# Where the queries of a dilated attention kernel are put into block order, and how early

## The chip, the cores and the metric

The kernel runs on one core of one Trainium2 chip. The metric is the device time of one execution in microseconds. Names of the engines: PE is TensorE (matmuls; PEld its weight loads), DVE is VectorE, ACT is ScalarE, POOL is GpSimd, SP is SyncE, which here issues the DMAs. All data is float32. A measurement of this kernel can tell a difference of about 0.3% from no change.

## What is computed

One layer of a decoder with two attention mixers side by side, for a prompt of 2048 tokens and 8 single sample tokens. What matters here is mixer A on the prompt: each of 8 heads is evaluated in three strided patterns, and the three partial outputs are merged by their softmax denominators. Mixer B is an ordinary window of 128 (dilation 1) with a learned sink per head.

```python
DILATED_CONFIGS = ((128, 1), (512, 4), (2048, 16))

def _band_partial(q, k, v):
    # q, k, v cut into blocks of 128; each block of queries sees its own and the previous block of keys
    sc = jnp.einsum('nbqhgd,nbkhd->nbhgqk', qb, kk) * (HEAD_DIM ** -0.5)
    sc = jnp.where(valid[None, :, None, None], sc, -jnp.inf)
    m = sc.max(-1)
    p = jnp.exp(sc - m[..., None])
    den = p.sum(-1)
    o = jnp.einsum('nbhgqk,nbkhd->nbqhgd', p, vv).reshape(n, L, hk, g, dh)
    ...
    return m, den, o

def _prompt_layer(x, w_in, sinks, w_o, ln_g, ln_b):
    ...
    qa, ka, va, ga, qb, kb, vb, gb = _project(x, pos, w_in)
    parts = []
    for _, d in DILATED_CONFIGS:
        m, den, o = _band_partial(_dilate(qa[:, :, :, None], d), _dilate(ka, d), _dilate(va, d))
        parts.append((_undilate(m, b, s, d), _undilate(den, b, s, d), _undilate(o, b, s, d)))
    oa = _merge(parts)
    ...
    y = _output(x, oa, ob, ga, gb, w_o, ln_g, ln_b)
```

## The kernel before

The kernel runs in three stages. Up to about 400 us it projects keys, part of the queries and the values. Then comes the attention stage, which the change touches, up to about 1000 us. At the end stands the output projection with its normalization.

**Batches.** The attention stage works on pairs of heads: four pairs of mixer A, then four of mixer B. A pair of A has three jobs, with dilation 16, 4 and 1; a pair of B has one, with dilation 1. A job has 16 blocks of 128 queries, worked on in four batches of four blocks. That makes 16 jobs and 64 batches, numbered 0 to 63 here: 0 to 3 are dilation 16 of the first pair, 4 to 7 its dilation 4, 8 to 11 its dilation 1, 12 to 15 dilation 16 of the second pair, and so on; 48 to 63 are mixer B.

**Queries in block order.** A pair's queries lie in SBUF as a tile `q` of 128 x 2048, loaded by four DMAs (L906), in an order of tokens that suits dilation 16. For that dilation the scores read `q` directly. For dilations 4 and 1 the queries of a batch are first copied into a tile `qo` of 128 x 512, in the order of the blocks; this is `fetch_q` (L789 to L801), with the copy itself in L800. There are two buffers of `qo`. So 48 of the 64 batches need such a copy.

**A pipeline of batches, in an order written out by hand.** In step i of the loop at L1121 come the scores of batch i on PE (L823), the products with the values of batch i-2 (L874), the masked minimum (L831, DVE) and the exponential (L834, ACT) of batch i, and, in four slots, the transposes of batch i-1 (L853, PE) with their evictions `pT` (L859 on DVE, each fourth on ACT). Into the slots PE's remaining work is strewn by `advance`: projections of the gates and of mixer B's queries (L629), later the first part of the output projection. In slot 1 of step i stands `fetch_q` for batch i+1 (L1143). Each engine gets its instructions in the order in which this code issues them (`manual_schedule`), SP with its DMAs too.

**POOL in this stage.** When the third job of a pair of A is done, `merge_a` (L1001) joins the three partial outputs in eight chunks of 256 tokens. Each chunk needs a tile `F` of three weights, spread over 64 partitions each, which two DMAs fetch from DRAM (L1038); `F` has two buffers. A chunk is five instructions on POOL (one L1050, two each of L1052 and L1053), and between chunks lie two slots, in which the fetch for the chunk after next is issued. The merge of a pair falls into the steps of the next pair's dilation 4 and 1. POOL also splits weights into a high and a low part (L137, L138: `gw`, `gw2h`, `gw3h`, `wl`, `wo`), for which it waits for their loads and for the last matmul that read the buffer, and it copies the sample tokens' gates (L174, `sgS`).

**SP in this stage** issues in order: `F`, the projection's inputs `gx` (L581), keys, queries and values of the next job (L898, L906, L772 to L782), weights (L142), and the stores of gates (L175), queries (L200) and merged outputs (L1058).

Of the kernel before, what the change touches and what calls it, by code (L numbers as in the profile page):

```python
# [51 lines left out]
def hymba_step(ctx, tc, xt, xs, xr, wq, wv, wo, tab, msk, ident, diag, sinks, lng, lnb,  # L52
               kca, vca, kcb, vcb, y, kto, vo):
    nc = tc.nc
    V, S, G, T = nc.vector, nc.scalar, nc.gpsimd, nc.tensor
# [37 lines left out]
    def tick(last=False):  # L93
        slot[0] += 1
        raw_step()
        while due and (last or any(d.at <= slot[0] for d in due)):
            now = [d for d in due if last or d.at <= slot[0]]
            due[:] = [d for d in due if d not in now]
            for d in now:
                d.run()  # L100
# [125 lines left out]
    with tc.tile_pool(name="wp", bufs=2) as wp, tc.tile_pool(name="pw", bufs=2) as pw:  # L226
# [13 lines left out]
        def x_of(ci, kt):  # L240
            return [t[:, kt % 2] for t in X5[kt // 2]] if ci == 6 else [t[:, kt] for t in X[ci]]
# [248 lines left out]
    with xscope, tc.tile_pool(name="spa", bufs=1, reuse_waits="tile") as sp, \  # L490
# [9 lines left out]
        for gi, (h0, w) in enumerate(VG):  # L500
            wvh, wvl = wvp[gi]
            for tb in VO[gi]:
# [3 lines left out]
                if gi == 1 and nt in (26, 30):  # L506
                    i = (nt - 26) // 4
# [14 lines left out]
                for kt in () if new else range(8):  # L522
                    ci = max(i for i in range(7) if CHUNKS[i][0] <= tb * 128)
                    t0 = tb * 128 - CHUNKS[ci][0]
                    a, b = [t[:, t0:t0 + 128] for t in x_of(ci, kt)]
# [229 lines left out]
    class Job:  # L755
# [33 lines left out]
        def fetch_q(self, g):  # L789

            q = self.of.q
            if self.d == 16:
                self.Q[g] = q[:, g * 512:g * 512 + 512]
                return
            o = at.tile([128, 512], F32, name="qo", bufs=2)
            if self.d == 4:
                a, b = o.rearrange("p (b j i) -> p b j i", b=4, j=4), q.rearrange("p (j r b i) -> p r b j i", j=4, r=4, b=4)[:, g]
            else:
                a, b = o.rearrange("p (b r i) -> p b r i", b=4, r=16), q.rearrange("p (r b i) -> p b r i", r=16, b=16)[:, 4 * g:4 * g + 4]
            V.tensor_copy(a, b)  # L800
            self.Q[g] = o  # L801

        def keys(self, n):
# [121 lines left out]
    def statistics(job):  # L925

        pst = ps.tile([128, 512], F32, name="pst", tag="pt", bufs=1)
        T.transpose(pst[:64, :128], job.of.st[:, job.si].rearrange("p a b c -> p (a b c)"), idt)
        stT = at.tile([64, 128], F32, name="stT")
        V.tensor_copy(stT, pst[:64, :128])  # L930
        yield
        for h in range(2):
            sd = job.of.sd[h, job.si]
            if job.d == 16:
                dma(sd.rearrange("k (n p) -> (k n) p", n=16), stT[32 * h:32 * h + 32])
                continue
            for kind in range(2):
                src = stT[32 * h + 16 * kind:32 * h + 16 * kind + 16]
                if job.d == 4:
                    dma(sd[kind].rearrange("(j n i) -> n j i", j=4, n=16), src.rearrange("n (j i) -> n j i", j=4))  # L940
                else:
                    dma(sd[kind].rearrange("(r b i) -> b r i", r=16, b=16), src.rearrange("n (r i) -> n r i", r=16))
# [126 lines left out]
    def advance(ns):  # L1069

        nonlocal debt
        debt += ns
        while debt > 0:
            t = next(follow, None)
            if t is None:
                debt = 0.0
                break
            debt -= t

    pairs = [Pair(p, isb) for isb in (False, True) for p in range(4)]  # L1080
    jobs = [j for p in pairs for j in p.jobs]
    starts = [4 * jobs.index(p.jobs[0]) for p in pairs]
    N = 4 * len(jobs)
# [8 lines left out]
    def step():  # L1092

        tick()
        for todo in (chains, fetches):
            while todo and next(todo[0], 1):
                todo.pop(0)

    def prefetch(i):
        p, what = loads.get(i, (None, None))  # L1100
        if what == "k":
            if p.isb and p.pair % 2:
                p.k = pairs[pairs.index(p) - 1].k
            else:
                fetches.append(load_k(p))
        elif what == "q":
            while p.isb and len(queries) < 24:
                next(follow)
            fetches.append(load_q(p))
        if i % 4 == 2 and i // 4 + 1 < len(jobs):  # L1110
            fetches.append(jobs[i // 4 + 1].fetch_v())
        if i in spare:
            late_wo(spare[i])

    with tc.manual_schedule(engines=set(ENGINES)):
        steady.append(True)
        pairs[0].k, pairs[0].q = first["k"], first["q"]
        jobs[0].vals.append(first["v"])
        V.tensor_scalar(mk, mk, -1.0, None, op0=OP.mult)
        jobs[0].fetch_q(0)  # L1120
        for i in range(N + 2):  # L1121
            new, mid, old = [jobs[k // 4] if 0 <= k < N else None for k in (i, i - 1, i - 2)]
            if new:
                if i in starts:
                    new.of.begin()
                new.scores(i % 4)
            if old:
                old.values((i - 2) % 4)
            if new:
                new.weights(i % 4, range(6))  # L1130
            if old:
                old.evacuate((i - 2) % 4)
                if (i - 2) % 4 == 3 and old.last:
                    chains.append(merge_b(old) if old.of.isb else merge_a(old))
            if new:
                prefetch(i)
            nb = len(mid.banks(0)) if mid else 0
            for sl in range(4):
                if mid and sl * nb % 4 == 0:
                    mid.turn((i - 1) % 4, sl * nb // 4)  # L1140
                if new and sl < 2:
                    new.weights(i % 4, (6 + sl,))
                if sl == 1 and i + 1 < N:  # L1143
                    jobs[(i + 1) // 4].fetch_q((i + 1) % 4)
                where[0] = sl
                advance(RATE / 4 if i else RATE / 2)
                step()
            if mid and (i - 1) % 4 == 3 and not mid.of.isb:
                stat = statistics(mid)
                next(stat)  # L1150
                chains.append(stat)
        while chains or fetches:
            advance(RATE / 4)
            step()
        tick(True)
        steady.clear()
# [179 lines left out]
```

## Time and profile before

| what | us |
|---|---|
| median of 3 runs | 1212.94 |
| the runs | 1209.42, 1213.45, 1212.94 |
| the profiled execution | 1207.77 |
| its span in the profile | 1206.0 |
| PE busy in the span | 1139.4 |
| DVE busy | 549.5 |
| ACT busy | 430.9 |
| POOL busy | 353.3 |

The profile is of one execution. Its first page gives the span, the busy time of each engine, the chain of work that ended last, and the costliest groups of instructions: line of the code, engine, operation, output tile <- input tile, shape, count, then busy us and mean ns of one, then the idle time of the engine just before them and what ended it. In a timeline a row is start, length, engine, line, operation, count, and in brackets the idle time before it with the instruction that ended it. Views by stretches of time give each engine's busy time (PE, PEld, DVE, ACT, POOL), the granted clock of TensorE, the share of DMA and GB/s. Numbers behind tile names are left out in the profile. A tile's wait for several semaphores is put down to the one that came last.

### The profile page before, as it was taken

To read this page: it belongs to the slowest core of one execution; us is meant where nothing else is said; L and a number is where in the kernel's file an instruction comes from. 1 tells how busy PE (TensorE), PEld (TensorE's weight loads), DVE (VectorE), ACT (ScalarE), POOL (GpSimd) and SP (SyncE) were. 2 spreads that over 40 slices of the span, in tenths; PEclk is the share of its full clock that TensorE was granted. 3 is DMA by queue.
4 is the path that set the end of the run, shared out by engine and by line. 5 is a ranking of instruction groups with operands and counts; after the bars stand their busy time and mean duration, and the time that the engine had idled before them with its cause. 6 is when DMAs were issued, how large, how long until landed. Compare 5 with 4: busy or idle time off the path is not lost.

```text
span 1206.0 us, 23406 instructions
## 1 busy us (share of the span) xinstructions
PE 1139.4 (94%) x8614; PEld 997.6 (83%) x8614; DVE 549.5 (46%) x1787; ACT 430.9 (36%) x1417; POOL 353.3 (29%) x470
## 2 busy tenths in 40 slices
PE   8999999999989999999999899998899896999997
PEld 7899999987978888988897788877677774688885
DVE  6532001011002565555566547555666665675444
ACT  3200011101102565555555445555455451132221
POOL 2243011120002100044605302460254443276332
PEclk9999999999999999999999999999999999999998
DMA  8845898284596475558767846868887767555521
GB/s 273 264 131 161 255 292 265 92 241 155 167 303 204 142 201 169 132 140 204 229 161 178 223 138 166 207 149 221 186 221 219 250 193 208 170 187 190 188 85 70
DMA packets 206066, 230.14 MB, mean 191 GB/s; under 512 B 34640, under 2 KB 174576, under 8 KB 205568
## 3 DMA queue, kind: packets, MB, share of 16 engines
q1 hardware_dynamic: 205952, 228.66, 65.5%
q8 instruction: 67, 1.10, 0.4%
q14 instruction: 47, 0.39, 0.1%
HBM read 158.52 MB, written 70.07 MB: 190 GB/s over the span
## 4 chain that ended last, share of the span: by engine, by line
PE 71%; DMA 12%; DVE 6%; ACT 5%; issue 3%; POOL 2%; SPq 2%; DVEq 0%; POOLq 0%; ACTq 0%
PE po L672 13%; PE pg L629 12%; PE pv L527 8%; PE ps_s L823 7%; PE ps_pt L853 6%; PE ps_o L874 5%; PE ppt L152 5%; PE pmm L152 5%; PE ps L152 5%; ACT pe L834 3%; DMA gx<-xd 3%; PE po L152 3%; DMA F<-fd 3%; DVE pT L859 2%; DVE sm L831 1%
## 5 line engine op out<-in xcount | busy, mean ns | idle before, releaser
L834 ACT ACTIVATE pe<-sm,st 128x256 f32<-128x256 f32 (+1 forms) x512 | 235.6, 461 | 217.3 <-DVE st L831 216.3
L831 DVE CUSTOM_DVE_ANT_0 sm<-ps_s,mk 128x256 f32<-128x256 f32 (+1 forms) x512 | 180.2, 375 | 152.2 <-PE ps_s L823 141.5
L629 PE MATMUL pg<-gx,gw 128*128 128x256 f32 (+1 forms) x1104 | 165.6, 291 | 7.5 <-DMA gx<-xd 4.5
L853 PE MATMUL ps_pt<-idt,pe 128*128 128x128 f32 x848 | 139.2, 284 | 24.5 <-DVE pT L859 23.8
L629 PEld LDWEIGHTS pg<-gx,gw 128*128 128x128 f32 x1104 | 140.8, 189 | 9.3 <-DMA gx<-xd 5.6
L859 DVE COPY pT<-ps_pt 128x512 f32<-128x512 f32 x176 | 121.2, 689 | 32.7 <-PE ps_pt L853 30.6
L853 PEld LDWEIGHTS ps_pt<-idt,pe 128*128 128x128 f32 x848 | 90.2, 140 | 48.2 <-DVE pT L859 34.2
L1050 POOL TENSOR_TENSOR oT<-oT,F 128x256 f32<-128x256 f32 x32 | 23.8, 745 | 341.6 <-ACT pe L834 178.0
L874 PE MATMUL ps_o<-pT,v 128*64 128x128 f32 (+1 forms) x1120 | 106.5, 334 | 0.0
L874 PEld LDWEIGHTS ps_o<-pT,v 128*64 128x64 f32 x1120 | 70.0, 137 | 39.3 <-issue 16.8
L834 ACT ACTIVATION_READ_ACCUMULATOR pe<-sm,st 128x1 f32 x512 | 95.8, 187 | 0.0
L823 PE MATMUL ps_s<-k,qo 64*128 64x256 f32 (+1 forms) x768 | 92.7, 381 | 0.0
L823 PEld LDWEIGHTS ps_s<-k,qo 64*128 64x128 f32 x768 | 67.4, 189 | 12.8 <-issue 1.8
L629 PE MATMUL pg<-gx,gw2h 128*128 128x256 f32 (+1 forms) x368 | 74.7, 291 | 1.6 <-ACT spe L406 1.6
L527 PE MATMUL pv<-wvh,xh 128*128 128x384 f32 (+1 forms) x224 | 69.5, 310 | 0.0
L527 PE MATMUL pv<-wvh,xl 128*128 128x384 f32 (+1 forms) x224 | 69.5, 310 | 0.0
L527 PE MATMUL pv<-wvl,xh 128*128 128x384 f32 (+1 forms) x224 | 69.4, 310 | 0.0
L672 PE MATMUL po<-wl,mho 128*128 128x512 f32 x192 | 59.7, 392 | 0.0
L629 PEld LDWEIGHTS pg<-gx,gw2h 128*128 128x128 f32 x368 | 57.8, 189 | 1.8 <-ACT spe L406 1.8
L539 ACT ACTIVATE vf<-pv 128x384 f32<-128x384 f32 (+1 forms) x32 | 14.0, 438 | 111.7 <-PE pv L527 58.1
L629 PE MATMUL pg<-gx,gw2l 128*128 128x256 f32 (+1 forms) x184 | 53.6, 292 | 0.0
L172 DVE SCALAR_TENSOR_TENSOR th<-th,pg 128x256 f32<-128x256 f32 (+1 forms) x64 | 26.9, 420 | 51.4 <-ACT th L168 51.0
(262 smaller groups left out, 2459.3 us busy)
## 6 DMA issues: line engine op xcount, KB each, us to landing
gx<-xd SPq DMA_DIRECT2D x80, 512.0 KB
F<-fd SPq DMA_DIRECT2D x80, 192.0 KB
gs<-th SPq DMA_DIRECT2D x64, 128.0 KB
v<-vs SPq DMA_DIRECT2D x28, 256.0 KB
xd<-xh SPq DMA_DIRECT2D x12, 512.0 KB
xd<-xl SPq DMA_DIRECT2D x12, 512.0 KB
kc<-in_kca SPq DMA_DIRECT2D x8, 768.0 KB
vc<-in_vca SPq DMA_DIRECT2D x6, 1024.0 KB
```

The lines of the kernel that those rows point to most:

```text
L152: T.matmul(p[:, :n], a[:, kt, :], b, start=k == 0, stop=k == 23)
L172: V.scalar_tensor_tensor(th[:, :n], th[:, :n], 1.0, p, op0=OP.add, op1=OP.mult)
L527: T.matmul(p[:, :w], l, r[:, kt, :w], start=k == 0, stop=k == 23)
L629: T.matmul(p[:, :n], a[:, kt, :], b[:, kt % 2, :n], start=kt + e == 0, stop=kt == 7 and e == 2)
L672: T.matmul(p, a, b[:, nh * 4:nh * 4 + 4].rearrange("p a b -> p (a b)"), start=first and k == 0, stop=last and k == end)
L823: T.matmul(s[:, h, n % 4, :w], self.Q[g][r, n % 4 * 128:n % 4 * 128 + 128], self.keys(n)[r], start=True, stop=True)
L831: V.tensor_tensor_reduce(sm[:, :w], self.s[:, h, n % 4, :w], mk[:, MI[self.d], 256 - w:], -0.125, 3.0e38, op0=OP.add, op1=OP.min, accum_out=m)
L834: S.activation(p[:, :w], sm[:, :w], AF.Exp, scale=-1.0, bias=m, accum_out=den)
L853: T.transpose(pt[:, h, j], self.P[h, n][:, a:a + 128], idt)
L859: V.tensor_copy(t, pt)
L874: T.matmul(o[64 * h:64 * h + 64, a:a + 128 * len(ns)], v[:, cv, kv:kv + 64], t[:, h, j:j + len(ns)].rearrange("p a b -> p (a b)"), start=n ...
L1050: G.tensor_mul(m, m, F[:, 0])
```

## The change

```diff
             if self.d == 4:
                 a, b = ...
             else:
                 a, b = ...
-            V.tensor_copy(a, b)
+            G.tensor_copy(a, b)
             self.Q[g] = o
...
         jobs[0].fetch_q(0)
+        jobs[0].fetch_q(1)
         for i in range(N + 2):
...
-                if sl == 1 and i + 1 < N:
-                    jobs[(i + 1) // 4].fetch_q((i + 1) % 4)
+                if sl == 1 and i + 2 < N:
+                    jobs[(i + 2) // 4].fetch_q((i + 2) % 4)
```

The copy into block order goes from DVE (`V`) to POOL (`G`), and is issued in slot 1 of step i for batch i+2, no longer for batch i+1. The two buffers of `qo` stay: the copy for batch i+2 takes the buffer that the scores of batch i have read at the start of the step. `fetch_q(1)` ahead of the loop issues no instruction, since job 0 has dilation 16.

What this moves shows in the engines' orders. First DVE, in the step of batch 19, where the copy for batch 20 stood (`sm` and `st` are the masked scores and their minimum, `pT` the eviction of transposed weights, `th` a gate). Before:

```order
L831 ISA sm,st_5258<-ps_s,mk 128x256
L831 ISA st_5258 128x1
L800 COPY qo<-q 128x512
L859 COPY pT<-ps_pt 128x512
L172 SCALAR_TENSOR_TENSOR th<-th,pg 128x256
```

Now:

```order
L831 ISA sm,st_5258<-ps_s,mk 128x256
L831 ISA st_5258 128x1
L859 COPY pT<-ps_pt 128x512
L172 SCALAR_TENSOR_TENSOR th<-th,pg 128x256
L831 ISA sm,st_5258<-ps_s,mk 128x128
```

The copy is gone, and the eviction stands right behind the minimum; so at all 48 places.

Then POOL, in the merge of the first pair, chunks six and seven (`oT` with a number is one dilation's output, `F` the weights of a chunk). Before:

```order
L1050 TENSOR_TENSOR oT_4080<-oT_4080,F 128x256
L1052 TENSOR_TENSOR F<-oT_4545,F 128x256
L1053 TENSOR_TENSOR oT_4080<-oT_4080,F 128x256
L1052 TENSOR_TENSOR F<-oT_5047,F 128x256
L1053 TENSOR_TENSOR oT_4080<-oT_4080,F 128x256
L1050 TENSOR_TENSOR oT_4080<-oT_4080,F 128x256
L1052 TENSOR_TENSOR F<-oT_4545,F 128x256
L1053 TENSOR_TENSOR oT_4080<-oT_4080,F 128x256
L1052 TENSOR_TENSOR F<-oT_5047,F 128x256
L1053 TENSOR_TENSOR oT_4080<-oT_4080,F 128x256
```

Now:

```order
L800 COPY qo<-q 128x512
L1050 TENSOR_TENSOR oT_4080<-oT_4080,F 128x256
L1052 TENSOR_TENSOR F<-oT_4547,F 128x256
L1053 TENSOR_TENSOR oT_4080<-oT_4080,F 128x256
L1052 TENSOR_TENSOR F<-oT_5049,F 128x256
L1053 TENSOR_TENSOR oT_4080<-oT_4080,F 128x256
L1050 TENSOR_TENSOR oT_4080<-oT_4080,F 128x256
L1052 TENSOR_TENSOR F<-oT_4547,F 128x256
L1053 TENSOR_TENSOR oT_4080<-oT_4080,F 128x256
L1052 TENSOR_TENSOR F<-oT_5049,F 128x256
L1053 TENSOR_TENSOR oT_4080<-oT_4080,F 128x256
L800 COPY qo<-q 128x512
```

The first copy is that for batch 20, between the fifth and the sixth chunk; the second is that for batch 21, between the seventh and the eighth. The copy for batch 22 stands behind the eighth.

Last POOL at the end of the third pair's merge, now (eighth chunk, then the split of a weight `gw`); before, the same rows stood there without the two copies:

```order
L800 COPY qo<-q 128x512
L1050 TENSOR_TENSOR oT_7150<-oT_7150,F 128x256
L1052 TENSOR_TENSOR F<-oT_7679,F 128x256
L1053 TENSOR_TENSOR oT_7150<-oT_7150,F 128x256
L1052 TENSOR_TENSOR F<-oT_8217,F 128x256
L1053 TENSOR_TENSOR oT_7150<-oT_7150,F 128x256
L174 COPY sgS<-th 128x8
L137 CAST gw_9484<-raw 128x256
L138 TENSOR_TENSOR gw_9484<-raw,gw_9484 128x256
L137 CAST gw_9484<-raw 128x256
L138 TENSOR_TENSOR gw_9484<-raw,gw_9484 128x256
L800 COPY qo<-q 128x512
```

The first is the copy for batch 45, the second that for batch 46, behind two of the eight parts of `gw`. PE's order is the same as before through the attention stage. On SP a few loads of the output stage (`gb`, `xo`, `mgp`) stand in another order.

## The prediction

> **What bounds the kernel now.** I read the first page first: the span and the chain that ended last. Then the busy time of each engine in stretches of 50 us (PE first after the length), for the part that the change touches.
>
> ```profile
> span 1206.0 us, 23406 instructions
> PE 71%; DMA 12%; DVE 6%; ACT 5%; issue 3%; POOL 2%; SPq 2%; DVEq 0%; POOLq 0%; ACTq 0%
> 550.00:600.00 50.00, 48.32 (x417) 41.16 (x417) 27.72 (x103) 26.93 (x98) 32.06 (x52) 1.00 0.77 207
> 650.00:700.00 50.00, 45.50 (x361) 37.05 (x360) 26.22 (x99) 24.52 (x90) 16.57 (x24) 0.93 0.86 242
> 750.00:800.00 50.00, 47.27 (x399) 40.03 (x398) 29.80 (x109) 27.37 (x100) 25.60 (x39) 1.00 0.71 177
> ```
>
> TensorE is the bound of the attention stage: in the three stretches it lacks 1.68, 4.50 and 2.73 us of 50, while DVE is a little over half busy. So little is to be won by relieving DVE, and anything that makes PE wait is added to the end almost in full. The POOL column is not small in these stretches (32 of 50 in the first): they are the merges of mixer A.
>
> **What is taken from DVE.** The copies `qo<-q` as a group (busy, mean ns), and their shortest, median and longest; then where PE waited for DVE between 400 and 1000 us.
>
> ```profile
> L800 DVE COPY qo<-q 128x512 f32<-128x512 f32 x48 | 24.2, 503 | 0.0
> L800 DVE COPY qo<-q x48: 414/423/1682, 409.4 to 978.5; 128x512 f32<-128x512 f32 x48
> PE ps_pt L853 <- DVE pT L859: 23.8, 34, 1.1
> ```
>
> 48 copies at 503 ns are 24.2 us of DVE. They count only where PE waits for the eviction `pT` that stands right behind one. I went through the 48 with the row that follows on DVE. In most, PE waits for nothing behind them. In nine, the next row (`th`, L172) then waits for ACT, so that the copy's time turns into a longer wait of DVE and nothing is won. Eight are left; of PE's rows there, first and last and two whose value differs:
>
> ```profile
> 568.83 0.44 PE L853 MATMUL ps_pt<-idt,pe 128*128 128x128 f32 x2 [0.15 <-DVE pT L859]
> 848.06 0.66 PE L853 MATMUL ps_pt<-idt,pe 128*128 128x128 f32 x4 [0.31 <-DVE pT L859]
> 937.15 0.66 PE L853 MATMUL ps_pt<-idt,pe 128*128 128x128 f32 x4 [0.81 <-DVE pT L859]
> 980.75 0.66 PE L853 MATMUL ps_pt<-idt,pe 128*128 128x128 f32 x4 [0.84 <-DVE pT L859]
> ```
>
> Each can give back the smaller of its wait and its copy: 0.15 + 0.31 + 0.81 (a long copy) + 5 x 0.42 (the median) = **3.4 us gained**. That is one end; the other is nothing, where PE's wait passes to ACT.
>
> **What a copy costs on POOL.** The trace has none of this shape there. The nearest rows: one input, 256 and 8 elements; two inputs, 512 elements.
>
> ```profile
> L137 POOL CAST gw<-raw 128x256 fp32r<-128x256 f32 x16 | 6.6, 412 | 2.6 <-DMA raw<-in_wq 2.6
> L174 POOL COPY sgS<-th 128x8 f32<-128x8 f32 x8 | 1.7, 217 | 14.2 <-DVE th L172 14.2
> L260 POOL TENSOR_TENSOR wl<-w,wh 128x512 fp32r<-128x512 f32 x18 | 24.2, 1361 | 83.8 <-DVE wh L259 83.8
> ```
>
> The line through the two one-input rows is 0.79 ns an element, so 512 elements take 412 + 256 x 0.79 = 0.61 us. I take 0.61, as it has one input; the ends are 0.41 (the half-size row) and 1.36 (two inputs at full size). [...]
>
> **Where the copies stand on POOL.** This decides. POOL's rows in the trace stand in the order of its program, so a copy starts only when the row ahead of it is done. That row is, in three of the four merges, one that waits for pieces `F` from DRAM. In the first merge (POOL rows with the idle time before them in brackets; PE rows are the starts of the scores):
>
> ```profile
> 552.30 0.73 POOL L1050 TENSOR_TENSOR oT<-oT,F 128x256 f32<-128x256 f32 x1 [8.81 <-DMA F<-fd]
> 555.32 0.74 POOL L1053 TENSOR_TENSOR oT<-oT,F 128x256 f32<-128x256 f32 x1
> 551.10 1.79 PE L823 MATMUL ps_s<-k,qo 64*128 64x128 f32 x16
> 564.94 0.74 POOL L1050 TENSOR_TENSOR oT<-oT,F 128x256 f32<-128x256 f32 x1 [3.35 <-DMA F<-fd]
> 567.97 0.80 POOL L1053 TENSOR_TENSOR oT<-oT,F 128x256 f32<-128x256 f32 x1
> 560.23 2.00 PE L823 MATMUL ps_s<-k,qo 64*128 64x256 f32 x16
> ```
>
> By the new order the copy for batch 20 stands behind the fifth chunk, whose last row ends at 555.32 + 0.74 = 556.06. With 0.61 the block is ready at 556.67, but PE began these scores at 551.10: PE waits 5.6 us. The copy for batch 21 stands behind the seventh chunk: 567.97 + 0.80 + 0.61 = 569.38 against 560.23, so PE is by then **9.15 us** late in all (lateness is the largest so far, not a sum). Two batches of lead, some 18 us (9.1 us between these two scores), are eaten by a merge whose chunks come slower than its program places them. The copy behind the eighth chunk finds PE already shifted and costs nothing more. Scores, values, transposes and projections all stand behind the waiting scores on PE; DVE and ACT then wait for PE.
>
> The second and third merge, by the copy that comes latest (batch 33, batch 46), and the row where POOL in turn waits for PE:
>
> ```profile
> 676.01 0.74 POOL L1053 TENSOR_TENSOR oT<-oT,F 128x256 f32<-128x256 f32 x1
> 669.75 2.00 PE L823 MATMUL ps_s<-k,qo 64*128 64x256 f32 x16
> 797.51 0.74 POOL L138 TENSOR_TENSOR gw<-raw,gw 128x256 fp32r<-128x256 f32 x1
> 793.58 2.00 PE L823 MATMUL ps_s<-k,qo 64*128 64x256 f32 x16
> 810.11 0.40 POOL L137 CAST gw2h<-raw 128x256 fp32r<-128x256 f32 x1 [2.99 <-PE ps_pt L853]
> 814.24 0.74 POOL L138 TENSOR_TENSOR gw2l<-raw,gw2h 128x256 fp32r<-128x256 f32 x1
> 815.05 1.79 PE L823 MATMUL ps_s<-k,qo 64*128 64x128 f32 x16
> ```
>
> Second: 676.75 + 0.61 - 669.75 = **7.6 us**. Third: 798.25 + 0.61 - 793.58 = 5.3; then the weight parts `gw2h` wait for PE, so they move with it, and the copy for batch 48 behind them ends at 814.98 + 5.28 + 0.61 = 820.87 against 815.05 + 5.28 = 820.33, another 0.5: **5.8 us**. Fourth, in mixer B, with the smallest margin of all its copies (batch 57):
>
> ```profile
> 910.45 0.74 POOL L1053 TENSOR_TENSOR oT<-oT,F 128x256 f32<-128x256 f32 x1
> 916.09 2.00 PE L823 MATMUL ps_s<-k,qo 64*128 64x256 f32 x16
> ```
>
> 4.9 us are left, and the copy takes 0.61 of it: nothing. The other copies stand where POOL is idle or has several microseconds; the merge rows that they push are covered by the waits for `F` in brackets above.
>
> What the stalls give back: behind the second merge PE waited for projection inputs, which SP can now fetch while PE stands.
>
> ```profile
> 689.57 0.97 PE L629 MATMUL pg<-gx,gw 128*128 128x256 f32 x6 [0.80 <-DMA gx<-xd]
> 691.91 0.79 PE L629 MATMUL pg<-gx,gw 128*128 128x256 f32 x2 [1.37 <-DMA gx<-xd]
> ```
>
> I take both, **2.2 us**; the other end is none. The last loads of the output stage (`gb`, `xo`, `mgp`) stand in another order on SP; PE has work for some time when they are issued, and I cost that at nothing, with 2 us either way.
>
> **The sum.** 9.15 + 7.6 + 5.8 = 22.6 us of stalls, less 3.4 and 2.2: +17.0 us. The profiled execution took 1207.77 us (span 1206.0), hence 1224.8. It lies 5.2 us under the median of the runs, 1212.94, and under the lowest of them, 1209.42; on the median's footing the forecast is **1230 us**.
>
> **Rivals.**
> *The stalls feed themselves.* SP also works in order, and some of its stores wait for what PE makes. In the first merge the fetch of the eighth chunk stands behind a store of projected queries, whose tile ACT evicts after PE:
>
> ```profile
> 558.19 0.36 ACT L182 ACTIVATE qf<-pg 128x256 f32<-128x256 f32 x1
> 561.54 0.54 SPq L200 DMA_DIRECT2D qb<-qf  x1
> 562.36 3.06 SPq L1038 DMA_DIRECT2D F<-fd  x2
> ```
>
> With PE 5.6 us late the tile is ready at 564.1 instead of 558.55, so the store and this fetch come 2.6 us later. I count it as hidden, since the copy behind it has about that margin. If each merge loses 2.6 us so, the four copies that count take 1.36 and not 0.61 (3.0 us), and nothing is given back by SP: 22.6 + 7.8 + 3.0 - 3.4 = +30, so 1243. For it: stores and fetches share one queue. Against: in the first two merges the latest copy precedes the delayed fetch.
>
> *Faster: DVE's relief reaches PE.* The place is mixer B, where PE waits for DVE most:
>
> ```profile
> PE ps_pt L853 <- DVE pT L859: 14.6, 19, 1.1
> ```
>
> 17 of the copies lie between 800 and 1000 us; if each shortens PE's path by 0.503 us, 8.6 of these 14.6 us go: 1204. It decides only if the copies are in time, that is if the fifth to seventh chunk of the first merge end 9.15 us earlier. The idle rows in front of those chunks (8.81 and 3.35) show that nearly all of their waiting for `F` would have to go, so little speaks for it. [...]
>
> *No change that can be measured.* The pieces land faster while PE stands, stalls shrink to the 8.9 us that PE lacks in the three stretches, and the gains of 3.4 and 2.2 stand against them: +3, so 1216.
>
> That the change does not do what it says is ruled out by the order of instructions: the 48 copies are POOL's, one batch earlier.
>
> **How the numbers follow.** Forecast 0.66, self-feeding stalls 0.20, no measurable change 0.08, faster 0.06. Low end: copies at 0.41 (-0.8), stalls a quarter smaller as `F` lands faster (-5.6), DVE's gain 8.6 and not 3.4 (-5.2): +5, which on the median's footing is 1218; I go to 1216 for the third rival. High end: 1243 and 2 for the output stage: 1245. A measurement of this kernel can tell 0.3% (3.6 us) from no change; faster by that 0.06, within it 0.07, slower 0.87.
>
> **What would show it.** Right: scores waiting for POOL `qo` by 5.6 and 3.6 us in the first merge (batches 20 and 21), by 7.6 us in all in the second, by 5.8 us in the third, none in mixer B; copies of about 0.6 us on POOL; DVE with 24 us less; PE's wait for `pT` down by some 3 us. Wrong: no wait of PE for `qo`, or waits spread over all batches; the prices would be wrong if copies took over 1 us, or if the chunks of a merge closed up while PE stood.

## The result and the profile after

The changed kernel took 1223.27 us in the median of 11 runs (1216.48 to 1228.36), the kernel before on the same chip 1212.94 (11 runs, 1209.28 to 1218.19). The ratio is 1.0094, with a 95% interval of 1.0069 to 1.0118: about 0.9%, or 10 us, slower.

From the first page of the changed kernel: span, share of the chain that ended last, and the groups of the copy and of the scores. Then rows of the view of waits (engine, what waited, what it waited for: us in all, times, longest).

```profile
span 1226.6 us, 23421 instructions
PE 63%; DMA 19%; DVE 5%; ACT 5%; issue 3%; POOL 3%; SPq 2%; DVEq 0%; POOLq 0%; ACTq 0%
L823 PE MATMUL ps_s<-k,qo 64*128 64x256 f32 (+1 forms) x768 | 95.6, 391 | 15.3 <-POOL qo L800 15.3
L800 POOL COPY qo<-q 128x512 f32<-128x512 f32 x48 | 29.1, 612 | 117.4 <-PE ps_s L823 98.9
PE ps_s L823 <- POOL qo L800: 15.3, 6, 5.4
PE ps_pt L853 <- DVE pT L859: 21.7, 31, 1.1
```

A copy takes 612 ns on POOL. PE, which never waited for `qo` before, now waits for it six times, 15.3 us in all, and in the chain DMA has grown from 12% to 19% at PE's expense: the chunks of the merge, behind which the copies stand, wait for DMA (POOL for `F` at L1050: 183.6 us, against 162.5 before). PE's wait for `pT` has shrunk by 2 us.

The same three stretches of 50 us as before (PE, PEld, DVE, ACT, POOL, then granted clock, DMA share, GB/s):

```profile
550.00:600.00 50.00, 43.24 (x340) 35.83 (x339) 22.89 (x84) 23.12 (x82) 34.26 (x57) 0.93 0.75 190
650.00:700.00 50.00, 42.50 (x335) 35.30 (x337) 22.19 (x83) 22.02 (x79) 25.67 (x38) 0.90 0.85 208
750.00:800.00 50.00, 42.03 (x349) 35.09 (x349) 23.54 (x94) 22.58 (x88) 22.95 (x33) 0.94 0.73 153
```

PE lacks 6.76, 7.50 and 7.97 us of 50 where it lacked 1.68, 4.50 and 2.73. And something in these rows was not in the prediction: the granted clock has fallen from 1.00, 0.93 and 1.00 to 0.93, 0.90 and 0.94. The timeline of the first merge shows what that means, POOL first (chunk five's first and last row, the copy for batch 20; chunk seven's last row, the copy for batch 21), then PE (scores of batch 20, the values behind them, scores of batch 21):

```profile
555.13 0.72 POOL L1050 TENSOR_TENSOR oT<-oT,F 128x256 f32<-128x256 f32 x1 [8.09 <-DMA F<-fd]
558.10 0.72 POOL L1053 TENSOR_TENSOR oT<-oT,F 128x256 f32<-128x256 f32 x1
558.76 0.61 POOL L800 COPY qo<-q 128x512 f32<-128x512 f32 x1
570.43 0.74 POOL L1053 TENSOR_TENSOR oT<-oT,F 128x256 f32<-128x256 f32 x1
571.11 0.61 POOL L800 COPY qo<-q 128x512 f32<-128x512 f32 x1
559.43 3.36 PE L823 MATMUL ps_s<-k,qo 64*128 64x128 f32 x16 [5.41 <-POOL qo L800]
562.72 3.02 PE L874 MATMUL ps_o<-pT,v 128*64 128x256 f32 x16
571.78 2.00 PE L823 MATMUL ps_s<-k,qo 64*128 64x256 f32 x16 [0.29 <-POOL qo L800]
```

The copy for batch 20 stands behind the fifth chunk, which waits 8.09 us for its `F`, and the scores wait 5.41 us for it (5.6 predicted). Then these 16 matmuls take 3.36 us; before, they took 1.79. The values behind them take 3.02 us, where in other batches and without a wait they take 1.73. That is 2.9 us more, and so PE reaches batch 21 late by itself, with a wait of 0.29 us left where 3.6 had been predicted. POOL sets the lateness, and slow matmuls use up what would have been the second wait. The chain that ended last shows this: it reaches the scores of batch 21 through the copy, the seventh chunk and its pieces `F`, and not through the slow matmuls (start, length, what; the rows between left out):

```profile
560.69 6.58 DMA F<-fd
570.43 0.74 POOL oT L1053
571.17 0.56 POOL qo L800
571.78 2.02 PE ps_s L823 x16
```

That the matmuls are slow by the clock shows in narrower stretches of the same view: the wait, the scores of batch 20, the values, what follows.

```profile
557.00:558.50 1.50, 0.00 (x0) 0.00 (x0) 0.00 (x0) 0.00 (x0) 1.42 (x3) 1.00 1.11 236
558.60:559.43 0.83, 0.00 (x1) 0.00 (x1) 0.00 (x0) 0.00 (x0) 0.78 (x2) 0.50 0.95 270
559.43:562.70 3.27, 3.27 (x16) 2.29 (x16) 0.00 (x0) 0.00 (x0) 1.81 (x3) 0.50 0.57 153
562.70:565.00 2.30, 2.30 (x14) 1.34 (x14) 2.10 (x12) 1.83 (x9) 1.74 (x3) 0.50 0.59 84
565.40:568.00 2.60, 2.60 (x26) 2.39 (x23) 1.23 (x4) 1.67 (x7) 0.59 (x1) 1.00 0.94 242
```

PE's last matmul before the wait ended at 554.02. The granted clock fell to 0.50 between 558.50 and 558.60, still within the wait, and was back at 1.00 by 565.40.

How late each batch's scores begin against the profile of before, with the start of batch 1 set to zero (us, worked out from the starts of L823; the second line is another profile of the same changed kernel, told below):

```
batch            19    20    21    31    32    33    36    43    44    45    46    48    49    63
changed        -0.7   5.4   8.6   7.8  14.4  16.8  11.9  11.9  16.8  19.7  20.0  20.0  16.9  14.7
changed again  -0.6   4.5   8.5   9.0  14.2  17.8  12.9  12.9  14.4  17.3  19.0  19.0  15.9  13.8
```

Three merges, three rises: 9.3, 9.0 and 8.1 us in the first line. After the second and the third come falls of 4.9 and 3.1.

### The profile page after: what moved, and what is told of

It is laid out like the page before. It is cut to its first block, busy times and chain, and to the rows that moved or that the text cites. A ratio compares the mean times of both kernels' runs of the same rounds, so it can differ in the third digit from the quotient of the medians.

```text
span 1226.6 us, 23421 instructions
## 1 busy us (share of the span) xinstructions
PE 1150.1 (94%) x8614; PEld 1005.6 (82%) x8614; DVE 529.1 (43%) x1739; ACT 431.0 (35%) x1417; POOL 378.4 (31%) x518
## 4 chain that ended last, share of the span: by engine, by line
PE 63%; DMA 19%; DVE 5%; ACT 5%; issue 3%; POOL 3%; SPq 2%; DVEq 0%; POOLq 0%; ACTq 0%
PE po L672 14%; PE pg L629 11%; PE pv L527 7%; PE ps_s L823 6%; DMA F<-fd 6%; PE ps_pt L853 5%; PE ps_o L874 4%; PE ps L152 4%; PE pmm L152 4%; PE ppt L152 4%; ACT pe L834 3%; DMA gx<-xd 3%; PE po L152 2%; DMA xin<-in_xt 2%; DVE pT L859 2%
## 5 line engine op out<-in xcount | busy, mean ns | idle before, releaser
L853 PE MATMUL ps_pt<-idt,pe 128*128 128x128 f32 x848 | 139.9, 285 | 22.2 <-DVE pT L859 21.7
L874 PE MATMUL ps_o<-pT,v 128*64 128x128 f32 (+1 forms) x1120 | 111.0, 344 | 0.0
L823 PE MATMUL ps_s<-k,qo 64*128 64x256 f32 (+1 forms) x768 | 95.6, 391 | 15.3 <-POOL qo L800 15.3
L1050 POOL TENSOR_TENSOR oT<-oT,F 128x256 f32<-128x256 f32 x32 | 23.4, 732 | 228.4 <-DMA F<-fd 183.6
L823 PEld LDWEIGHTS ps_s<-k,qo 64*128 64x128 f32 x768 | 69.2, 195 | 28.9 <-POOL qo L800 16.8
L800 POOL COPY qo<-q 128x512 f32<-128x512 f32 x48 | 29.1, 612 | 117.4 <-PE ps_s L823 98.9
```

Of the source, the lines that this page charges most:

```text
L800: G.tensor_copy(a, b)
L823: T.matmul(s[:, h, n % 4, :w], self.Q[g][r, n % 4 * 128:n % 4 * 128 + 128], self.keys(n)[r], start=True, stop=True)
L853: T.transpose(pt[:, h, j], self.P[h, n][:, a:a + 128], idt)
L874: T.matmul(o[64 * h:64 * h + 64, a:a + 128 * len(ns)], v[:, cv, kv:kv + 64], t[:, h, j:j + len(ns)].rearrange("p a b -> p (a b)"), start=n ...
L1050: G.tensor_mul(m, m, F[:, 0])
```

## The experiments

In the diffs `V` is DVE and `G` is POOL. "The change" is the kernel above; each ratio is to the kernel before, measured on the same chip beside it.

### The two halves of the change, each alone

`dve2` keeps the copy on DVE and takes only the lead of two batches; `pool1` puts it on POOL and keeps the lead of one.

```diff
 dve2 (from the change)
-            G.tensor_copy(a, b)
+            V.tensor_copy(a, b)
 pool1 (from the kernel before)
-            V.tensor_copy(a, b)
+            G.tensor_copy(a, b)
```

> The copies two batches ahead as in the change, but on VectorE. Queue theory (PE loses time only where a copy stands on GpSimd behind a late merge): no PE wait for qo, the time of before within 0.3% (ratio 0.997 to 1.003), since VectorE's work is the same and only one batch earlier. Rival (the lead itself costs, by the two buffers of qo or by the other order of the last loads on SyncE): 1.006 to 1.010, as with the change.

> On GpSimd, but one batch ahead as before. Queue theory: every copy stands about two merge chunks later on GpSimd, and by the trace of before the latest of each merge are 18.3, 17.9, 14.7 and 6.3 us late, 57 us in all; less some 10 us that other waits give back: +40 to +55 us, ratio 1.033 to 1.045. Rival (lead plays no part, the copies cost by themselves): 1.009 as with the change.

`pool1`: 1.0432 (1.0399 to 1.0464), as forecast. PE waits for `qo` in twelve waits:

```profile
PE ps_s L823 <- POOL qo L800: 55.4, 12, 10.4
```

So the engine is the harm, and the second batch of lead takes three quarters of it away.

`dve2`: 1.0047 (1.0023 to 1.0070), between the two forecasts, and no wait for `qo` at all. The lead alone was not free, though. DVE, SP and PE of `dve2` around 810 us:

```profile
810.64 0.43 DVE L800 COPY qo<-q 128x512 f32<-128x512 f32 x1 [8.22 <-DMA raw<-in_wq]
801.28 1.10 SPq L906 DMA_DIRECT2D q<-qb  x2
804.49 1.12 SPq L906 DMA_DIRECT2D q<-qb  x2
812.06 1.12 PE L853 MATMUL ps_pt<-idt,pe 128*128 128x128 f32 x4 [8.30 <-DVE pT L859]
```

This is the copy for batch 48, the first of mixer B. It reads queries whose loads SP issues only from 801.28 to 805.6. Issued a batch earlier, the copy stands in DVE's queue before they land; the eviction `pT` behind it is held, and PE waits 8.3 us. The bracket names another load, `raw`, which this copy doesn't read; the view puts down a wait to the DMA that came last. In the changed kernel POOL comes to this copy only at 832.88, behind the parts of a weight, and doesn't wait in front of it. There a wait for queries stands ahead of another copy, that of batch 52, the first of the next pair (at 862.84); PE's scores don't wait for it:

```profile
POOL qo L800 <- DMA q<-qb: 10.9, 1, 10.9
```

### Which of the 48 copies

If only the copies in the three merges are late, then a kernel with just those on POOL costs as much as the change, and one with just those on DVE costs nothing. Both have the lead of two.

```diff
+            LATE = {20, 21, 22, 23, 32, 33, 34, 35, 44, 45, 46, 47, 48}
+            n = 4 * jobs.index(self) + g
-            G.tensor_copy(a, b)
+            (V if n in LATE else G).tensor_copy(a, b)     # split
+            (G if n in LATE else V).tensor_copy(a, b)     # lateonly
```

> Two batches ahead; the 13 copies that stand behind or in the late part of a merge (batches 20 to 23, 32 to 35, 44 to 48) on VectorE, the other 35 on GpSimd. Queue theory: by the trace of before the tightest copy left on GpSimd (batch 31) is ready 1.6 us early, so no PE wait for qo, and VectorE's relief in mixer B stays: ratio 0.996 to 1.000. Rival (it is GpSimd's copies as such, by their contention with VectorE or by slower merges): most of the loss stays, 1.005 to 1.009.

> The complement: only the 13 copies of batches 20 to 23, 32 to 35, 44 to 48 on GpSimd, the other 35 on VectorE, two batches ahead. Queue theory: all stalls of the change (scores of batches 20, 21, 32, 33, 44, 45, 46 wait for qo) and none of its gain: ratio 1.009 to 1.014. Rival (copies on GpSimd cost in proportion to their number): 13/48 of the loss, 1.002 to 1.004.

`lateonly`: 1.0112 (1.0087 to 1.0136), as forecast, with five waits for `qo`:

```profile
PE ps_s L825 <- POOL qo L802: 16.3, 5, 5.6
```

These 13 copies carry the whole loss.

`split`: 1.0059 (1.0038 to 1.0080). The stalls were gone, with one wait for `qo` of 0.67 us left, but the forecast of 0.996 to 1.000 was missed, and the ratio lies in the range of the rival. The cause is another, though, the one that `dve2` showed: 48 is among the 13, and there DVE waits again for the queries of mixer B. Counted as in the table above, the batches up to 46 begin at most 3.2 us late, and 10.1 us come in one step, at batch 47.

```profile
812.38 0.43 DVE L802 COPY qo<-q 128x512 f32<-128x512 f32 x1 [9.46 <-DMA raw<-in_wq]
```

### The lead without batch 48, and the two engines mixed

```diff
-                if sl == 1 and i + 2 < N:
-                    jobs[(i + 2) // 4].fetch_q((i + 2) % 4)
+                if sl == 1:
+                    for k in (i + 1, i + 2):
+                        if k < N and k - i == (1 if k in LATE else 2):
+                            jobs[k // 4].fetch_q(k % 4)
```

This is how both differ from the change in their lead. `dve2b`: all copies on DVE, `LATE` is {48}, so only this copy keeps the old lead. `mixed`: the 13 copies as before the change (DVE, one batch ahead), the other 35 as after it (POOL, two ahead).

> All copies on VectorE two batches ahead, but that of batch 48, the first of mixer B, one batch ahead as before. In the trace of the kernel with all copies on VectorE two ahead, this copy held VectorE for 8.2 us until its queries had landed, and PE waited 8.3 us. Theory (this one wait is the whole cost of the longer lead): ratio 0.998 to 1.002. Rival (the lead costs elsewhere too): 1.003 to 1.005.

> The 13 copies of batches 20 to 23, 32 to 35 and 44 to 48 on VectorE one batch ahead as before, the other 35 on GpSimd two batches ahead. Queue theory: no copy is late, none waits for queries that have not landed, and VectorE is relieved of 15 copies in mixer B, where PE waits for it: ratio 0.996 to 0.999. Rival (GpSimd's copies cost by themselves, or VectorE's relief does not reach PE): 1.000 to 1.004.

`dve2b`: 1.0021 (1.0000 to 1.0043), between its two forecasts, against 1.0047 for `dve2`. The two were run beside different runs of the kernel before and their intervals overlap, but the profile is plain: PE's longest wait for `pT` is 1.1 us again, not 8.3. A lead of two costs little or nothing once that copy is left where it was.

`mixed`: **0.9972** (0.9948 to 0.9996), 1207.79 us in the median of 12 runs against 1211.94. No wait for `qo`. It is faster than both kernels, by an interval that only just leaves 1 out. What it wins, 0.28% or 3.4 us, should be the relief of DVE without the stalls. Its profile shows a part of that:

```profile
PE ps_pt L855 <- DVE pT L861: 21.3, 32, 1.1
PE pg L630 <- DMA gx<-xd: 6.8, 7, 2.2
```

PE waits 21.3 us for `pT`, against 23.8 and 23.5 in the two profiles of the kernel before, but 6.8 us for `gx`, against 4.5 and 5.8. From the start of batch 1 to that of batch 63 it needs 591.1 us, against 592.2 and 591.6. So at most 1.1 of the 3.4 us shows in the one profile, and that all of it is DVE's relief is likely, but not shown.

### One more batch of lead

If POOL is late by the wait of one chunk, a third batch of lead should cover it. To make room for a third buffer of `qo`, both kernels have less elsewhere (`sm` two buffers and not three, three raw weight buffers and not four). `pool3` has the lead of three in mixer A; `pool2c`, the control, is the change with the smaller buffers.

```diff
 pool3
-            o = at.tile([128, 512], F32, name="qo", bufs=2)
+            o = at.tile([128, 512], F32, name="qo", bufs=3)
...
+                    for k in (i + 2, i + 3):
+                        if k < N and k - i == (2 if jobs[k // 4].of.isb else 3):
+                            jobs[k // 4].fetch_q(k % 4)
 both
-                sm = at.tile([128, 256], F32, name="sm", bufs=3)
+                sm = at.tile([128, 256], F32, name="sm", bufs=2)
-RAW = 4
+RAW = 3
```

> All copies on GpSimd, three batches ahead in mixer A (two in mixer B) with three buffers of qo; room for the third by two buffers of sm and three of raw instead of three and four. Queue theory: by the trace of before every copy is ready 0.8 us or more ahead of its scores, so no wait for qo, ratio 0.997 to 1.002 (against the control with the same buffers and the lead of the change: 0.006 to 0.012 lower). Rival (the stalls are not a matter of lead, since a merge that comes late is late by any lead): as the control.

> Control for the one with three batches of lead: the change itself with two buffers of sm and three of raw instead of three and four. Expected like the change, 1.007 to 1.014; what lies above that is the price of the buffers.

`pool2c` gave 1.0302 (1.0272 to 1.0331), `pool3` 1.0186 (1.0164 to 1.0209). Both missed their ranges, but PE waits for `qo` 13.7 us in `pool2c` and not at all in `pool3`, and the ratios differ by 0.0116, as forecast. So the lateness is a matter of lead, as a queue would have it. As a repair it is worthless here, because the smaller buffers alone cost 2% (PE waits 39.3 us for `pT` in `pool2c` and 21.7 in the change).

### The chunks sooner

The other way round: fetch the weights `F` two slots sooner, so that the chunks ahead of the copies come sooner.

```diff
 merge_a, in the loop over chunks c
+            if c < 6:
+                fetch(c + 2)
             yield
             yield
-            if c < 6:
-                fetch(c + 2)
```

> The change, with one edit: in the merge of mixer A the fetch of the weights F for the chunk after next is issued before the two slots that lie between chunks, not behind them. If the copies are late because the chunks of a merge come slower than their places in the program (each waits for a fetch that is issued two slots before it), the chunks come earlier, the waits of the scores for qo shrink to under 8 us in all (23 with the change), and the ratio to the kernel before falls from 1.009 to 1.001-1.006. Rival: the fetches are held by the queue's throughput or by what SP issues ahead of them, not by the place where they are issued; then the waits stay at 18-25 us and the ratio at 1.007-1.012.

Measured: 1.0081 (1.0050 to 1.0113). Each theory was half right. The waits for `qo` are gone but for 0.6 us (in the change they were 15.3 us, not 23), and the time has not moved, because another wait stands in their place. PE's waits of this kernel, then the first merge again:

```profile
PE pg L629 <- DMA gx<-xd: 15.7, 5, 4.1
PE ps_s L823 <- POOL qo L800: 0.6, 1, 0.6
556.01 0.47 PE L629 MATMUL pg<-gx,gw 128*128 128x256 f32 x2 [2.52 <-DMA gx<-xd]
560.23 1.43 PE L629 MATMUL pg<-gx,gw 128*128 128x256 f32 x5 [3.05 <-DMA gx<-xd]
561.59 2.98 PE L823 MATMUL ps_s<-k,qo 64*128 64x128 f32 x16
```

The `F` fetches now stand ahead of projection inputs `gx` in SP's order, and what the copies gained the inputs lost: 15.7 us against 1.7 in the change. In the view of SP's queue, two loads of `gx` that were issued at 548.73 and 550.12 in the change come at 555.94 and 557.18. Whether SP itself was held by a busy `F` buffer or the pieces shared the DMA engines, this run doesn't tell.

### Why the matmuls behind a wait are slow

`warm` lets PE work through most of the wait: 20 matmuls whose results are overwritten stand in front of the scores of batches 20, 32 and 44.

```diff
+            if 4 * jobs.index(self) + g in (20, 32, 44):
+                for u in range(20):
+                    T.matmul(s[:, u % 2, u // 2 % 4, :128], idt, mk[:, 0, :128], start=True, stop=True)
```

> The change, with 20 additional matmuls of 128x128 in front of the scores of batches 20, 32 and 44 (the identity by a piece of the mask, into the bank of the scores, overwritten by the scores), so that PE works through some 2-3 us of the 4-5 us in which it would wait there. Theory: the scores and values behind a long wait took twice as long (3.36 for 1.79, 3.02 for 1.73) because PE had stood idle. Then these scores take 1.8-2.1 us, and since the copy for the next batch is as late as before, the wait that was 0.29 at batch 21 grows to 2.5-3.6; the time stays within 0.3% of the change (ratio 1.006-1.012). Rival: the scores are slow for a reason of their own there (a shared port or bank while POOL copies and merges); then they stay at 3-3.4 us and the wait at batch 21 below 1 us, and the ratio rises to 1.009-1.014.

The additional matmuls, the scores and values of batch 20, the scores of batch 21:

```profile
555.73 4.63 PE L821 MATMUL ps_s<-mk,idt 128*128 128x128 f32 x40
562.07 1.79 PE L826 MATMUL ps_s<-k,qo 64*128 64x128 f32 x16 [1.71 <-POOL qo L800]
563.79 1.73 PE L877 MATMUL ps_o<-pT,v 128*64 128x256 f32 x16
575.28 3.78 PE L826 MATMUL ps_s<-k,qo 64*128 64x256 f32 x16 [4.00 <-POOL qo L800]
```

They ran for 4.63 us rather than 2 to 3. Behind them the scores took 1.79 us and the values 1.73, as they do without a wait. The second wait came back, at 4.00 us, near the 3.6 of the prediction, and now it is the scores of batch 21 that are slow. The clock in the stretches of the additional matmuls, of scores and values of batch 20, and of the scores of batch 21:

```profile
555.73:560.36 4.63, 4.63 (x42) 4.44 (x40) 0.00 (x0) 0.00 (x0) 2.52 (x4) 1.00 1.01 234
562.07:565.50 3.43, 3.43 (x33) 2.40 (x33) 1.59 (x9) 1.26 (x6) 2.52 (x4) 1.00 0.46 124
575.28:579.00 3.72, 3.72 (x18) 2.55 (x18) 0.00 (x0) 0.00 (x0) 1.82 (x3) 0.50 0.82 273
```

POOL works in all three, so it is not POOL's work that makes scores slow. Standing idle made PE's matmuls slow here (scores of 3.36 us behind 5.41 us of it in the change, of 1.79 behind 1.71 us in `warm`), and PE is late by what POOL sets, however the time until then is filled. The ratio is 1.0119 (1.0075 to 1.0163), within the forecast and within that of the rival; with four runs it can't be told from the change.

### Both kernels profiled again

> The changed kernel again, for another profiled execution: the first profile was of the slowest of its 11 runs (1228.36 us), that of the kernel before of the fastest of its 11. If the size of the stalls varies from one execution to the next, this profile shows waits of the scores for qo that differ by several us in at least one merge from 5.41, 4.30 and 4.72, and its time lies near its median of 1223. If the stalls are fixed by the order, the waits agree within 0.5 us and only the rest of the span differs. The ratio should be 1.007-1.012 either way.

> The kernel before again, for a second profiled execution: the first one was 5 us below its median. Expected: a time of 1209-1216 us, no wait of the scores for qo over 0.5 us, and 1-5 us more of PE's waiting for DMA in the attention stage than in the first profile.

`after2`: 1226.18 us (median of 7), ratio 1.0093 (1.0061 to 1.0124), profiled at 1226.44. The waits for `qo`:

```profile
PE ps_s L823 <- POOL qo L800: 17.7, 6, 5.0
569.27 3.10 PE L823 MATMUL ps_s<-k,qo 64*128 64x256 f32 x16 [2.23 <-POOL qo L800]
790.09 1.79 PE L823 MATMUL ps_s<-k,qo 64*128 64x128 f32 x16 [1.46 <-POOL qo L800]
802.00 3.68 PE L823 MATMUL ps_s<-k,qo 64*128 64x256 f32 x16 [2.80 <-POOL qo L800]
```

Single waits vary from one execution to the next (4.72 at batch 44 in the first profile, 1.46 here, and 2.80 at the next batch); the lateness that a merge adds varies less, by up to 2 us (the table above). `before2` took 1212.85 us. From the start of batch 1 to that of batch 63 it needed 591.6 us, and the first profile of before 592.2: the 5.1 us between these two executions lie outside the attention stage, 1.9 ahead of it and 3.7 behind. PE waited 1.3 us more for `gx`, as forecast, without a longer stage. The changed kernel needed 606.9 and 606.0 us there.

## Why the prediction was right, and where its sizes were off

The forecast was 1230 us and the range 1216 to 1245; the median came out at 1223.27. The mechanism is shown: copies in POOL's order behind chunks that wait for `F`, in three merges. `pool1` and `pool3` show that the lead decides, `lateonly` that the 13 copies carry the loss, `mixed` that it goes when these 13 go back. That the number came so near is in part luck: the stalls were larger than their terms, and what they gave back was larger still. In mixer B nothing waited for `qo`, as forecast.

**Price of the copy.** 0.61 predicted, 0.612 measured: the line through the two one-input rows held.

**The stalls.** The terms were 9.15, 7.6 and 5.8. Measured: 9.3, 9.0 and 8.1 in the first profile, 9.1, 8.8 and 6.1 in the second (batch 19 to 21, 31 to 33, 43 to 46): 26.4 and 24.0 us, not 22.6. The first term was right in size, but not in what fills it: PE waits 5.41 and 0.29 us there, not 5.6 and 3.6, and slow matmuls take most of the second wait's place. The step "lateness is the largest so far, not a sum" held. The scores of batches 21 and 33 in both profiles, and of batch 46 in the first, begin within 0.1 us of the end of POOL's copy. In the second merge (the last row of chunk seven, the copy for batch 33, its scores):

```profile
688.13 0.74 POOL L1053 TENSOR_TENSOR oT<-oT,F 128x256 f32<-128x256 f32 x1
688.81 0.61 POOL L800 COPY qo<-q 128x512 f32<-128x512 f32 x1
689.48 2.00 PE L823 MATMUL ps_s<-k,qo 64*128 64x256 f32 x16 [0.38 <-POOL qo L800]
```

What was mis-sized is the time of the chunks. The prediction took it from the trace of before, as if a merge came later by just what PE was late when it began. In the first merge that is so. In the second, chunk seven ends 9.2 us later than before (10.2 in the second profile), while PE was 7.8 (9.0) late at batch 31; in the third, chunk eight ends 14.8 us later (13.2), while PE was 11.9 (12.9) late at batch 43. These slips of 1.4 and 1.2 us, then 2.9 and 0.3, are nearly all that the terms 7.6 and 5.8 lack. Why the chunks slip isn't shown. Slow matmuls add to the lateness that a merge leaves only where the next copy is in time, in the second profile: 1.0 us from batch 21 to 22, and 0.6 at batch 46. The 0.5 us for batch 48 did not come: its copy ended 4.5 us ahead of its scores.

**What is given back.** 2.2 us were taken, 8.0 came (4.9 after the second merge, 3.1 after the third). Both are waits of the kernel before for `gx`, together with what they entailed. Before, at batch 35 and ahead of batch 49:

```profile
692.63 3.79 PE L823 MATMUL ps_s<-k,qo 64*128 64x256 f32 x16
823.73 0.98 PE L629 MATMUL pg<-gx,gw 128*128 128x256 f32 x6 [1.42 <-DMA gx<-xd]
827.05 0.62 PE L629 MATMUL pg<-gx,gw 128*128 128x256 f32 x3 [0.64 <-DMA gx<-xd]
```

The first row stands right behind the two waits that the prediction counted: the scores take 3.79 us there (granted clock 0.50) and 2.00 otherwise, so these waits cost about 5 us and not 2.2. The second group of waits was overlooked; from batch 48 to 49 it cost 3.1 us (12.7 us before, 9.6 in the change). In the change PE waits 1.7 us for `gx` in all, where it waited 4.5.

**The relief of DVE.** 3.4 us predicted. PE's wait for `pT` fell from 23.8 and 23.5 us to 21.7 and 20.2 in the pairs of profiles, and `mixed`, which has this gain without the stalls, measured 3.4 us faster (0.5 to 6.3 by its interval). DVE's busy time fell by 20.4 and 17.1 us, not by 24. From the start of batch 49 to that of batch 63, in mixer B, the changed kernel needs 152.8 and 153.0 us and `mixed` 151.3, the kernel before 155.0 and 153.7. The size fits, but two profiles of the kernel before differ there by 1.3 us, and `dve2`, without the relief, needs 153.1; so the gain isn't told apart from that.

**The sum and the footing.** In the attention stage the change cost 14.7 and 13.8 us by the profiles, against +17.0: the stalls were 3.8 and 1.4 us above their sum, and 5.8 us more were given back. The 5.2 us added for the footing were right: `before2` lay on the first median, with the same attention stage. The reordered loads at the end show no cost clear of the scatter: from the start of batch 63 to the end it is 226.2 and 227.4 us with the change, 223.2 and 226.9 before. But the medians differ by 10.3 and 11.8 us, 4.4 and 2.0 us less than the attention stages of the profiled executions. That remainder is open; no profile of a run shows where it goes.

**The rivals.** Stalls that feed themselves (1243) did not come in that size: the merges cost 24 to 26 us where that rival needed 33, and 8 us were given back; the slips of the chunks above may be a small part of it. Faster by DVE's relief (1204) falls, since its condition, copies in time, was not met; and `mixed`, where it was met, gained 0.28%, not the 0.7% of that rival. No measurable change (1216) falls with the interval, which begins at 1.0069; its condition, pieces that land faster while PE stands, was not met either, as the chunks came no sooner. A rival that was missing is a new wait by the lead itself: the copy of batch 48 waits for queries. It doesn't show in the change, where POOL comes to that copy late, and on DVE it costs about 6 us: in `dve2` the batches behind it are late by 8.9 us, of which 3.1 are given back.

## What to carry to other kernels

Where an engine works its rows in the order of its program, as POOL did here (the copy for batch 20 at 558.76, behind the fifth chunk's last row at 558.10, behind a wait of 8.09 us), a moved step costs what stands ahead of it: find the row that it queues behind, and ask what that row waits for, at each place and not on the average. Thirteen of 48 copies made the whole loss here, and leaving those where they were turned a loss of 0.9% into a gain of 0.3% (0.04 to 0.52%). And when PE is made to wait, read its other waits on the same stretch: some of them vanish (PE's 4.5 us for `gx` became 1.7 here), and one is worth more than its bracket says if the matmuls behind it are slow (the two behind the second merge about 5 us and not 2.2).

## What the runs showed of the hardware

In the attention stage, these waits of 2.9 us or more on PE were followed by slow matmuls, whatever PE waited for. In the change's first profile waits of 5.41, 4.30 and 4.72 us for `qo` stood ahead of scores of 3.36 us, at a granted clock of 0.50, where scores of this shape take 1.79 without a wait (at the 4.30 the clock was already at 0.50 when the wait began, behind one of 1.40 us for `gx`). In `after2` 5.04 and 4.85 us stood ahead of scores of 3.25 and 3.36, in `pool1` 3.03 and 9.28 ahead of 2.84 and 3.36. In `before2` a wait of 3.21 us for `gx` slowed six projections (1.65 us for 0.97) and the scores behind them (3.36), in `fearly` one of 3.05 five projections (1.43 for 0.86) and the scores (2.98). In `dve2` the transposes behind 8.30 us for `pT` took 1.12 us for 0.66. Behind the waits of 5.41 and 4.72 us the clock of 0.50 lasted 5.9 and 6.0 us, and in the first merge it added 2.9 us to the wait.

Waits between 1.4 and 2.8 us went either way: in `after2` 1.46 left the scores at 1.79 us, 2.23 and 2.80 were followed by scores of 3.10 and 3.68 us (2.00 without a wait), and in `warm` behind one of 2.77 they took 2.00. In the kernel before, two waits of 0.80 and 1.37 us with 1 us of work between them were followed by scores of 3.79 us at a granted clock of 0.50. `warm` shows the cause in the first merge to be the idle time: with PE at work for 4.63 us and a wait of only 1.71 us left, the clock was 1.00 and the scores took 1.79 us. How much idle time it takes isn't shown: 2.23 us were enough once, and 2.77 were not. In stretches of 50 us the low granted clock shows only as 0.90 to 0.94; in a stretch as long as the slow row it shows as 0.50.
